# Biases in two buffers, and a block-recursive solve queued behind the last maxima and under high priority, in a two-layer transformer kernel

## The chip, the cores and the metric

One Trainium2 chip, one of its cores. The time is what the device takes for one execution of the program, in microseconds (us); runs of one program are compared by their median. The engines of a core run side by side, each through its own list of instructions and in that list's order: TensorE (PE, with its weight loads PEld), VectorE (DVE), ScalarE (ACT), GpSimd (POOL) and SyncE (SP, which here only issues transfers). They wait for each other by semaphores.

## What is computed

Two blocks, on 256 positions of width 1024. The first block has a pooling layer and a stick-breaking attention layer, each with a memory attention and a gated feed-forward network. The second block is the part that the change touches. It projects its input to columns, of which some feed a block attention with a distance bias ("moba"), some an RWKV recurrence, and some two gates:

```python
u = _rms_norm(h, g_pre[i])
cols = u @ w_in[i]
...
y_a = _moba_attention(qa, ka, va, rel_bias) * silu(za)
y_b, z_b = _rwkv7_time_mix(b_cols, ...)
y_b = y_b * silu(z_b)
merged = (sigmoid(gate_a) * (y_a @ p_a[i]) + sigmoid(gate_b) * (y_b @ p_b[i]))
y = merged @ w_out[i]
h = h + _rms_norm(y, g_post[i])
h = h + sigmoid(h @ w_ple_gate[i]) * (p[i] @ w_ple_up[i])
```

The recurrence, `state = state * w + (state @ a) b + v k`, read out by `r`, is defined step by step over the 256 positions; its output goes through a norm over each head.

## The kernel before

The positions are two tiles of 128 (t = 0 and t = 1). Each tile's whole path is a Python generator (`stream`), and `advance` and `follow` take a step of one or the other in turn, so that both tiles use a block of weights while it is on the chip. A block of weights (`granule`, 256 rows of 512 columns) is loaded by SP into `raw` (four buffers), split by ACT into a rounded part `whi` (line 219) and by DVE into the rest `wlo` (line 220); three matmuls of 512 columns (lines 233 to 235, `acc`) then do one product in full precision. So PE can go on only if DVE and ACT keep splitting, and SP loads the next block only when DVE has read the old one.

The recurrence is done in blocks and not step by step. `rwkv` is a third generator, `side`, of which `aside` takes two steps for each step of tile 0 once the shifted columns are done. It forms strictly lower triangular matrices, one for each head (`rwkv_base`, PE at line 1048); their 32x32 diagonal blocks go through DRAM to POOL, which inverts them all in 30 steps of a multiplication and an addition (`rwkv_blocks`, lines 1069 and 1070), and come back through DRAM as `X` (line 1113). `rwkv_inverse` transposes `X` on DVE into `Z` (lines 1115 and 1116) and joins the 32x32 inverses into 64x64 ones (PE at 1122 and 1130, copies at 1125 and 1132). `rwkv_solve` then solves with them (1188, 1194, 1200) and adds the parts of the output (1208 to 1241), and `rwkv_out` is the norm (1248 to 1261), whose result `yr` is needed by the product with `p_b`.

The block attention (`moba`) runs once for each tile and within it for two groups of four heads. A group loads its distance biases (line 891), forms four tiles of scores (PE, 901), adds biases and takes the row maxima (DVE, 902), negates the maxima (903), takes exponentials (ACT, 906), transposes (PE, 911), copies (912), multiplies by the values (PE, 917) and scales (921).

The order of the instructions on each engine is set by a scheduler that goes by the order of the program, by priority, and by its own estimate of when inputs are there. A wait of an instruction holds up everything behind it on its engine. `behind(a, b)` asks for `a` to stand after `b`, without a wait.

Of the kernel before, what the change touches and what calls it, by code (L numbers as in the profile page):

```python
# [3 lines left out]

# [6 lines left out]
F32 = mybir.dt.float32  # L11
# [9 lines left out]
P = 128  # L21
# [60 lines left out]
def tile_kernel(ctx: ExitStack, tc: tile.TileContext, I, const, off, out):  # L82
# [220 lines left out]
    def close_pool(name):  # L303
        s_ = left if left and left[-1][0] == name else right
        assert s_[-1][0] == name, (name, s_)
        s_.pop()[1].close()
# [3 lines left out]
    def pool_of(name, side="left"):  # L310
        if name not in pools:
            pools[name] = open_pool(name, side)
        return pools[name]
# [345 lines left out]
    def second(t):  # L659
# [121 lines left out]
            V.scalar_tensor_tensor(gt, gt, 1.0, acc, op0=ALU.add, op1=ALU.mult)  # L781
        merged = gates["ga"]
        if t == NT - 1:
            close_pool("moba")
        yield f"out{t}"
        split_yB()
# [51 lines left out]
    def rwkv():  # L838

        el, eo = pools["elem"], pools["eo"]  # L840
        c = {}
        c["kkc"] = bcast(el, I["k_k_2"][0], 512, "kkc")
        c["kac"] = bcast(el, I["k_a_2"][0], 512, "kac")
        for nm, wn, bn in (("wup", "w_up_2", "w0_2"), ("aup", "a_up_2", "a0_2")):
            c[nm] = el.tile([65, 512], F32, name=nm)
            SP.dma_start(c[nm][:64], I[wn][0])
            SP.dma_start(c[nm][64:65], I[bn])
        c["cinc"] = cload(el, "cinc")
        c["half"] = cload(el, "half")
        for t in range(NT):  # L850
            yield from rwkv_elem(t, el, eo, c)
        close_pool("elem")
        close_pool("rk")
        co = pool_of("core")
        ST = co.tile([P, 4, HD], F32, name="ST")

        shared["mask"] = co.tile([P, 2, P], F32, name="mask")
        for w, op in enumerate((ALU.is_gt, ALU.is_ge)):
            G.affine_select(shared["mask"][:, w], one.to_broadcast([P, P]), pattern=[[1, P]], base=0,
                            channel_multiplier=-1, compare_op=op, fill=0.0)  # L860
        for t in range(NT):
            rwkv_base(t, co)
            yield
        rwkv_blocks(co)

        for t in range(NT):
            for tok in zip_longest(*[rwkv_factors(t, g, co) for g in range(2)]):
                if "turn" not in tok:
                    yield
            yield from rwkv_sides(t, co, ST)  # L870
        for _ in zip_longest(*[rwkv_inverse(t, co) for t in range(NT)]):
            yield
        for _ in zip_longest(*[rwkv_solve(t, co, ST) for t in range(NT)]):
            yield
        for t in range(NT):
            yield from rwkv_out(t, co)
            flags.add(f"out{t}")
        close_pool("core")
        close_pool("eo")
        flags.add("core")  # L880

    def moba(t, mo):
        ns = P * (t + 1)
        s0 = P * (1 - t)
        kT_, va = shared["bkT"], bva
        den = sm.tile([P, 8], F32, name="bden")
        mx = sm.tile([P, 8], F32, name="bmx")
        for g in range(2):

            bias = mo.tile([P, 4, T], F32, name="bias")  # L890
            SP.dma_start(bias, bass.AP(tensor=sk.tensor, offset=sk.offset + 127 + g * TOEP,
                                        ap=[[PITCH - 1, P], [2 * TOEP, 4], [1, T]]))
            pm = bias[:, :, s0:]

            for h in range(4):
                hh = 2 * h + g
                o = 64 * g
                if h % 2 == 0:
                    sc = ptr.tile([P, 512], F32, name="tr")
                sv = sc[:, (h % 2) * 256:(h % 2) * 256 + ns]  # L900
                PE.matmul(sv, bq[t][o:o + 64, h], kT_[o:o + 64, h, :ns], start=True, stop=True)
                V.tensor_tensor_reduce(pm[:, h], sv, pm[:, h], 1.0, -3e38, ALU.add, ALU.max, mx[:, hh:hh + 1])
            V.tensor_scalar(mx[:, g:8:2], mx[:, g:8:2], -1.0, None, op0=ALU.mult)
            for h in range(4):
                hh = 2 * h + g
                S.activation(pm[:, h], pm[:, h], AF.Exp, bias=mx[:, hh:hh + 1], accum_out=den[:, hh:hh + 1])
            pT = mo.tile([P, 2, 4, P], F32, name="bPT")
            for j in range(t + 1):
                ps = ptr.tile([P, 512], F32, name="tr")
                for h in range(4):  # L910
                    PE.transpose(ps[:, h * P:(h + 1) * P], pm[:, h, j * P:(j + 1) * P], ident)
                (S.copy if j else V.tensor_copy)(pT[:, j], ps.rearrange("p (a b) -> p a b", a=4))
            po = ptr.tile([P, 512], F32, name="tr")
            for h in range(4):
                hh = 2 * h + g
                for j in range(t + 1):
                    PE.matmul(po[:, h * HD:h * HD + HD], pT[:, j, h], va[j][:, hh * HD:hh * HD + HD],
                              start=(j == 0), stop=(j == t))
            rd = sm.tile([P, 4], F32, name="brd")
            V.reciprocal(rd, den[:, g:8:2])  # L920
            V.tensor_mul(by[t].rearrange("p (h two d) -> p h two d", h=4, two=2)[:, :, g],
                         po[:, :256].rearrange("p (h d) -> p h d", h=4), rd[:, :, None].to_broadcast([P, 4, HD]))
        V.tensor_mul(by[t], by[t], sza[t])
# [183 lines left out]
    def rwkv_inverse(t, co):  # L1107

        d = E[t]
        X = co.tile([P, 8, 32], F32, name="X", bufs=2)  # L1110
        Z = d["Z"] = co.tile([P, 8, 64], F32, name=f"Z{t}")
        G.memset(Z, 0.0)
        G.dma_start(X, of_rows(xsk[t]))
        for n in range(0, P, 64):
            V.transpose(Z[n:n + 32, :, 0:32], X[n:n + 32])
            V.transpose(Z[n + 32:n + 64, :, 32:64], X[n + 32:n + 64])
        yield
        T1 = co.tile([P, 8, 32], F32, name=f"Ld{t}")
        pt = aux(t)
        for h in range(8):  # L1120
            for n in range(0, P, 64):
                PE.matmul(pt[n:n + 32, h * 32:h * 32 + 32], d["Lc"][n + 32:n + 64, h], Z[n + 32:n + 64, h, 32:64],
                          start=True, stop=True)
        for n in range(0, P, 64):
            (S.copy if n else V.tensor_copy)(T1[n:n + 32], pt[n:n + 32, :256].rearrange("p (a b) -> p a b", a=8))
        yield
        px = aux(t)
        for h in range(8):
            for n in range(0, P, 64):
                PE.matmul(px[n:n + 32, h * 32:h * 32 + 32], X[n:n + 32, h], T1[n:n + 32, h], start=True, stop=True)  # L1130
        for n in range(0, P, 64):
            (S.copy if n else V.tensor_copy)(Z[n:n + 32, :, 32:64], px[n:n + 32, :256].rearrange("p (a b) -> p a b", a=8))
        yield
# [8 lines left out]
    def rwkv_sides(t, co, ST):  # L1142

        d = E[t]
        v = vz[t]
        d["rhs"] = co.tile([P, 8, HD * (t + 1)], F32, name=f"rhs{t}")
        if t:
            pa = aux(1)
            for h in range(4):
                PE.transpose(pa[:, h * P:(h + 1) * P], d["AR"][:, h, 0], ident)  # L1150
            S.copy(d["rhs"][:, :, HD:].rearrange("p (g h) e -> p h g e", g=2),
                   pa.rearrange("p (h g e) -> p h g e", h=4, g=2))
        pr = aux(0)
        for k in range(8):
            PE.matmul(pr[:, k * HD:k * HD + HD], d["KM", k // 4][:, k % 4, 0], v[:, head_cols(k)], start=True, stop=True)
        S.copy(d["rhs"][:, :, :HD], pr.rearrange("p (k e) -> p k e", k=8))
        yield
        py = aux(1)
        for k in range(8):
            PE.matmul(py[:, k * HD:k * HD + HD], d["KM", k // 4][:, k % 4, 1], v[:, head_cols(k)], start=True, stop=True)  # L1160
        S.copy(yr[t].rearrange("p h g e -> p g h e"), py.rearrange("p (g h e) -> p g h e", g=2, h=4))
        yield
        if t == 0:
            pS = aux(0)
            for k in range(8):
                o = 64 * (k // 4)
                PE.matmul(pS[o:o + 64, (k % 4) * HD:(k % 4) * HD + HD], d["kt"][:, head_cols(k)], v[:, head_cols(k)],
                          start=True, stop=True)
            S.copy(ST, pS[:, :256].rearrange("p (a b) -> p a b", a=4))
            yield  # L1170
# [104 lines left out]

    def aside(n):

        return sum(1 for _ in zip(range(n), side))

    def advance(t):  # L1280

# [68 lines left out]
```

## Time and profile before

| | us |
|---|---|
| runs shown, median (lowest, highest) | 981.4 (980.11, 981.53) |
| the profiled execution, its own time | 978.99 |
| its span in the trace | 977.3 |
| PE busy in the span | 930.1 |
| DVE busy | 589.3 |
| ACT busy | 509.5 |
| POOL busy | 115.7 |

The trace has a row for each instruction: start, duration, engine, line, operation, what it writes and reads, and, in brackets, how long its engine stood idle before it and what ended that. A granted clock of 1.00 is PE's higher level (2.4 GHz), 0.50 its lower (1.2 GHz).

### The profile page before, as it was taken

The numbers are of one execution on the slowest core, as the hardware profiler recorded it, in microseconds if no ns is written. First come the engines' busy times: TensorE is split into PE (matmuls) and PEld (weight loads), VectorE is DVE, ScalarE is ACT, GpSimd is POOL, SyncE is SP. The second block draws the span as 40 slices with busy tenths as digits, with TensorE's granted clock in tenths as the row PEclk, the third lists the DMA queues.
The fourth block names the chain that finished last, engine by engine and source line by source line (L and its number), as shares of the span: only waits on it lengthen the run. The fifth ranks groups of instructions, "written<-read, shape, count | busy, mean of one in ns | idle before, by whom it ended". The sixth has DMA issues, their size and how long they took to land.

```text
span 977.3 us, 12773 instructions
## 1 busy us (share of the span) xinstructions
PE 930.1 (95%) x4594; PEld 728.2 (75%) x4594; DVE 589.3 (60%) x1002; ACT 509.5 (52%) x883; POOL 115.7 (12%) x220
## 2 busy tenths in 40 slices
PE   8999999999999999999999999798989939999998
PEld 5777788888887777778888888566667727877776
DVE  4754666656666555566656667455997522466864
ACT  5752655555556786665555555454466312435542
POOL 3000200000002000020000000611435840000000
PEclk9999999999999999999999999899999955979999
DMA  7652566565655523456555655555435321235551
GB/s 268 237 185 65 152 197 190 190 184 187 194 175 170 153 84 104 149 185 195 185 185 188 193 178 163 152 153 148 126 117 136 107 53 34 66 120 176 186 175 44
DMA packets 105855, 150.22 MB, mean 154 GB/s; under 512 B 6840, under 2 KB 61214, under 8 KB 105792
## 3 DMA queue, kind: packets, MB, share of 16 engines
q1 hardware_dynamic: 104836, 147.54, 48.0%
q0 software_dynamic: 384, 1.05, 0.5%
q10 hardware_dynamic: 572, 0.82, 0.4%
q8 instruction: 36, 0.59, 0.3%
q14 instruction: 27, 0.22, 0.1%
HBM read 146.24 MB, written 3.15 MB: 153 GB/s over the span
## 4 chain that ended last, share of the span: by engine, by line
PE 75%; POOL 7%; issue 6%; DVE 6%; ACT 3%; DMA 3%; SPq 0%; ACTq 0%; DVEq 0%; POOLq 0%
PE acc L233 16%; PE acc L234 15%; PE acc L235 15%; PE aux L233 5%; PE aux L234 5%; PE aux L235 5%; PE tr L274 2%; DVE wlo L220 2%; POOL Lb L1070 2%; POOL tb L1069 2%; POOL col L711 1%; PE aux L564 1%; POOL rs_w L155 1%; ACT whi L219 1%; DMA x<-in_x_dram 1%
## 5 line engine op out<-in xcount | busy, mean ns | idle before, releaser
L220 DVE SCALAR_TENSOR_TENSOR wlo<-raw,gcol,whi 128x512 fp32r<-128x512 f32 (+1 forms) x364 | 269.0, 768 | 126.9 <-ACT whi L219 126.3
L219 ACT ACTIVATE whi<-raw,gcol 128x512 fp32r<-128x512 f32 (+1 forms) x364 | 243.2, 709 | 182.7 <-PE acc L235 100.7
L233 PE MATMUL acc<-whi,fTh 128*128 128x512 f32 x352 | 141.7, 402 | 0.1
L234 PE MATMUL acc<-wlo,fTh 128*128 128x512 f32 x352 | 137.7, 391 | 1.4 <-DVE wlo L220 1.4
L215 DVE TENSOR_TENSOR wlo<-raw,whi 128x1024 fp32r<-128x1024 f32 x80 | 97.6, 1224 | 66.6 <-ACT whi L214 66.1
L235 PE MATMUL acc<-whi,fTl 128*128 128x512 f32 x352 | 136.9, 390 | 0.0
L214 ACT ACTIVATE whi<-raw 128x1024 fp32r<-128x1024 f32 x80 | 84.7, 1060 | 76.0 <-PE acc L235 71.7
L234 PEld LDWEIGHTS acc<-wlo,fTh 128*128 128x128 f32 x352 | 66.3, 188 | 14.3 <-DVE wlo L220 2.2
L235 PEld LDWEIGHTS acc<-whi,fTl 128*128 128x128 f32 x352 | 66.1, 188 | 14.2
L233 PEld LDWEIGHTS acc<-whi,fTh 128*128 128x128 f32 x352 | 66.1, 188 | 13.9 <-ACT fTh L263 1.4
L233 PE MATMUL acc<-whi,actTh 128*128 128x512 f32 x176 | 72.4, 414 | 1.1 <-ACT actTh L263 0.8
L234 PE MATMUL acc<-wlo,actTh 128*128 128x512 f32 x176 | 70.5, 401 | 0.1
L235 PE MATMUL acc<-whi,actTl 128*128 128x512 f32 x176 | 69.8, 399 | 0.1
L234 PE MATMUL aux<-wlo,hTh 128*128 128x512 f32 x176 | 68.8, 391 | 0.0
L235 PE MATMUL aux<-whi,hTl 128*128 128x512 f32 x176 | 68.7, 390 | 0.0
L233 PE MATMUL aux<-whi,hTh 128*128 128x512 f32 x176 | 68.6, 392 | 0.0
L234 PE MATMUL acc<-wlo,act20h 128*128 128x512 f32 (+1 forms) x104 | 42.7, 411 | 3.7 <-DVE wlo L220 3.7
L233 PE MATMUL acc<-whi,act20h 128*128 128x512 f32 (+1 forms) x104 | 44.6, 429 | 0.0
L233 PE MATMUL acc<-whi,act21h 128*128 128x512 f32 (+1 forms) x104 | 44.2, 425 | 0.0
L234 PE MATMUL acc<-wlo,act21h 128*128 128x512 f32 (+1 forms) x104 | 42.0, 404 | 0.0
L235 PE MATMUL acc<-whi,act21l 128*128 128x512 f32 (+1 forms) x104 | 41.8, 402 | 0.0
L235 PE MATMUL acc<-whi,act20l 128*128 128x512 f32 (+1 forms) x104 | 41.3, 397 | 0.0
(405 smaller groups left out, 1531.8 us busy)
## 6 DMA issues: line engine op xcount, KB each, us to landing
raw<-in_a_w_gu_dram SPq DMA_DIRECT2D x88, 256.0 KB, 3.2
raw<-in_b_w_gu_dram SPq DMA_DIRECT2D x88, 256.0 KB, 3.2
raw<-in_w_in_dram SPq DMA_DIRECT2D x44, 512.0 KB, 3.7
raw<-in_a_w_down_dram SPq DMA_DIRECT2D x22, 512.0 KB, 3.8
raw<-in_b_w_down_dram SPq DMA_DIRECT2D x22, 512.0 KB, 3.7
raw<-in_a_w_out_dram SPq DMA_DIRECT2D x8, 512.0 KB, 3.7
raw<-in_w_kv_dram SPq DMA_DIRECT2D x8, 512.0 KB
raw<-in_b_w_q_dram SPq DMA_DIRECT2D x8, 512.0 KB, 4.3
```

The costliest lines, as they stand in the source:

```text
L155: V.tensor_scalar(w, y, y, h, op0=ALU.mult, op1=ALU.mult)
L214: S.activation(hi[:, :m], raw[:, :m], AF.Copy)
L215: V.tensor_sub(lo[:, :m], raw[:, :m], hi[:, :m].bitcast(F32))
L219: shared["hi"] = S.activation(hi[:, a], raw[:, a], AF.Copy, scale=g)
L220: V.scalar_tensor_tensor(lo[:, a], raw[:, a], g, hi[:, a].bitcast(F32), op0=ALU.mult, op1=ALU.subtract)
L233: PE.matmul(acc, ah[:, k], wh[:, kk], start=first, stop=False)
L234: PE.matmul(acc, ah[:, k], wl[:, kk], start=False, stop=False)
L235: PE.matmul(acc, al[:, k], wh[:, kk], start=False, stop=last)
L274: PE.transpose(ps[:, c * P:(c + 1) * P], src[:, c * P:(c + 1) * P], ident)
L564: PE.matmul(z[:, h * P:(h + 1) * P], kT[j][o:o + 64, p0 + h], qT[t][o:o + 64, p0 + h], start=(h == 0), stop=False, skip_group_check=True)
L1069: G.tensor_mul(tv, Lb[:, j + 1:, j:j + 1].to_broadcast([64, n, j]), Lb[:, j:j + 1, :j].to_broadcast([64, n, j]))
L1070: G.tensor_add(Lb[:, j + 1:, :j], Lb[:, j + 1:, :j], tv)
```

## The change

Four things. The generator of the recurrence waits, ahead of its last part, until the second tile's last group of maxima has been written in the program; from there on every step taken by `aside` is under the scheduler's high priority. The eight transposes of `X` are put `behind` the negation of those last maxima. The second tile loads the biases of both groups at its start, the second group's into a buffer of its own in a new pool. That pool is closed ahead of the attention's.

```diff
         if t == NT - 1:
+            close_pool("bias")
             close_pool("moba")
...
             yield from rwkv_sides(t, co, ST)
+
+        while "maxima" not in shared:
+            yield
+        flags.add("urgent")
+        yield
         for _ in zip_longest(*[rwkv_inverse(t, co) for t in range(NT)]):
             yield
...
+        def bias_of(g):
+
+            bias = (pool_of("bias", "right") if t and g else mo).tile([P, 4, T], F32, name="bias")
+            SP.dma_start(bias, bass.AP(tensor=sk.tensor, offset=sk.offset + 127 + g * TOEP,
+                                       ap=[[PITCH - 1, P], [2 * TOEP, 4], [1, T]]))
+            return bias
+
+        both = [bias_of(g) for g in range(2)] if t else None
         for g in range(2):
-
-            bias = mo.tile([P, 4, T], F32, name="bias")
-            SP.dma_start(bias, bass.AP(tensor=sk.tensor, offset=sk.offset + 127 + g * TOEP,
-                                        ap=[[PITCH - 1, P], [2 * TOEP, 4], [1, T]]))
-            pm = bias[:, :, s0:]
+            pm = (both[g] if t else bias_of(g))[:, :, s0:]
...
-            V.tensor_scalar(mx[:, g:8:2], mx[:, g:8:2], -1.0, None, op0=ALU.mult)
+            last = V.tensor_scalar(mx[:, g:8:2], mx[:, g:8:2], -1.0, None, op0=ALU.mult)
+            if t and g:
+                shared["maxima"] = last
...
-            V.transpose(Z[n:n + 32, :, 0:32], X[n:n + 32])
-            V.transpose(Z[n + 32:n + 64, :, 32:64], X[n + 32:n + 64])
+            behind(V.transpose(Z[n:n + 32, :, 0:32], X[n:n + 32]), shared["maxima"])
+            behind(V.transpose(Z[n + 32:n + 64, :, 32:64], X[n + 32:n + 64]), shared["maxima"])
...
     def aside(n):
 
-        return sum(1 for _ in zip(range(n), side))
+        for _ in range(n):
+            with tc.high_priority() if "urgent" in flags else nullcontext():
+                if next(side, "end") == "end":
+                    return
```

Three places show what this does to the lists. Lines from 783 on have other numbers in the changed program: 902 is 912 there, 903 is 913, 912 is 924, 921 is 933, 1115 and 1116 are 1127 and 1128, 1188 is 1200, 1194 is 1206, 1200 is 1212, 1211 is 1223, 972 is 984, 979 is 991 and 991 is 1003.

The first is DVE's list at the first group of the second tile's maxima (`bmx` are the maxima, `Z_7174` the first tile's transposed inverses, `wlo` the split of a weight block). Before:

```order
L902 ISA bias,bmx<-tr,bias 128x256
L902 ISA bmx 128x1
L902 ISA bias,bmx<-tr,bias 128x256
L902 ISA bmx 128x1
L1115 STREAM_TRANSPOSE Z_7174<-X 32x8x32
L902 ISA bias,bmx<-tr,bias 128x256
L902 ISA bmx 128x1
L1116 STREAM_TRANSPOSE Z_7174<-X 32x8x32
L902 ISA bias,bmx<-tr,bias 128x256
L902 ISA bmx 128x1
L1115 STREAM_TRANSPOSE Z_7174<-X 32x8x32
L903 TENSOR_SCALAR bmx<-bmx 128x4
```

Now, from the end of that group on (its four maxima stand ahead of these rows):

```order
L913 TENSOR_SCALAR bmx<-bmx 128x4
L220 SCALAR_TENSOR_TENSOR wlo<-raw,gcol,whi 128x512
L932 RECIPROCAL brd<-bden 128x4
L924 COPY bPT<-tr 128x512
L933 TENSOR_TENSOR by_5582<-tr,brd 128x4x64
L220 SCALAR_TENSOR_TENSOR wlo<-raw,gcol,whi 128x512
L912 ISA bias,bmx<-tr,bias 128x256
...
L913 TENSOR_SCALAR bmx<-bmx 128x4
L1127 STREAM_TRANSPOSE Z_7197<-X 32x8x32
L1128 STREAM_TRANSPOSE Z_7197<-X 32x8x32
```

The transposes stood between the second and the third maximum of the first group; now they stand behind the second group's maxima, with the first group's copy, scaling and two weight splits ahead of them. The seven rows at the left out place are the read of that group's first maximum and its three other maxima with their reads.

The second place is PE's list in the solve (`rhs`, `Z`, `KM`, `Lb`, `N` are tiles of the solve, `acc` the gates' products). Before:

```order
L1188 MATMUL aux_7308<-rhs_6892,Z_7174 64x64 x8
L1188 MATMUL aux_7319<-rhs_7124,Z_7182 64x128 x4
L1188 MATMUL aux_7325<-rhs_7124,Z_7182 64x128 x4
L1194 MATMUL aux_7331<-KM_7307,N_6793 64x64 x4
L1194 MATMUL aux_7331<-KM_7307,N_6795 64x64 x4
L1194 MATMUL aux_7341<-Lb,N_7120 64x128 x4
L233 MATMUL acc<-whi,act21h 128x512
L234 MATMUL acc<-wlo,act21h 128x512
L1194 MATMUL aux_7347<-Lb,N_7122 64x128 x4
L235 MATMUL acc<-whi,act21l 128x512
```

Now:

```order
L1206 MATMUL aux_7356<-KM_7310,N_6793 64x64 x4
L1206 MATMUL aux_7356<-KM_7310,N_6795 64x64 x4
L1200 MATMUL aux_7322<-rhs_7127,Z_7205 64x128 x4
L1212 MATMUL aux_7378<-rhs_6892,Z_7197 64x64 x8
L1200 MATMUL aux_7328<-rhs_7127,Z_7205 64x128 x3
L1206 MATMUL aux_7366<-Lb,N_7123 64x128 x4
L1200 MATMUL aux_7328<-rhs_7127,Z_7205 64x128
L234 MATMUL acc<-wlo,act21h 128x512
```

The solve's third step (1200, now 1212) follows within the rows of its first two, where before ten `acc` matmuls stood ahead of it. Between the first matmul of the joins and the last of the solve stand 33 `acc` matmuls now and 36 before; from behind the second tile's first scores (901) to the first transposes of `by` (274) both lists hold the same 374 matmuls, 158 of them `acc`.

The third place is DVE's list some 60 us earlier, at the decays of the second tile (`ms` is the sum of two small vectors that the solve uses late). Before:

```order
L1005 TENSOR_REDUCE bon_6471<-sq 128x8
L220 SCALAR_TENSOR_TENSOR wlo<-raw,gcol,whi 128x512 x2
L1014 COPY AR_6502<-aux_6505 128x4x128
L220 SCALAR_TENSOR_TENSOR wlo<-raw,gcol,whi 128x512 x2
L1211 TENSOR_TENSOR ms_7406<-mid_6144,mid_6399 128x16
L220 SCALAR_TENSOR_TENSOR wlo<-raw,gcol,whi 128x512 x2
```

Now:

```order
L991 COPY mid_6399<-aux_6394 128x16
L1003 SCALAR_TENSOR_TENSOR k_6439<-k_6439,rk_5584 128x512
L1223 TENSOR_TENSOR ms_7431<-mid_6144,mid_6399 128x16
L984 TENSOR_TENSOR prev<-aux_6385,col 128x512
L1009 TENSOR_TENSOR bt<-bt,col 128x512
L220 SCALAR_TENSOR_TENSOR wlo<-raw,gcol,whi 128x512
```

The sum now stands two rows behind the copy that it needs; its exponential (line 1212) moves the same way on ACT. On SP's list, the second group's biases move ahead of four weight loads that stood before the first tile's second biases.

## Rows read from the trace of the kernel before

**Rows 1.** The page: span, busy time of PE, its clock in 40 slices.

```profile
span 977.3 us, 12773 instructions
...
PE 930.1 (95%) x4594; PEld 728.2 (75%) x4594; DVE 589.3 (60%) x1002; ACT 509.5 (52%) x883; POOL 115.7 (12%) x220
...
PEclk9999999999999999999999999899999955979999
```

**Rows 2.** Busy time by stretch: length, PE, PEld, DVE, ACT, POOL, granted clock, DMA share, GB/s.

```profile
782.60:800.00 17.40, 0.50 (x11) 0.37 (x11) 2.88 (x10) 0.68 (x3) 9.97 (x23) 0.59 0.12 30
800.00:826.70 26.70, 26.70 (x94) 21.04 (x95) 7.38 (x21) 8.27 (x23) 0.00 (x0) 0.50 0.20 59
826.70:857.40 30.70, 30.70 (x351) 25.46 (x349) 14.10 (x23) 12.03 (x21) 0.00 (x0) 1.00 0.24 70
857.40:867.60 10.20, 10.20 (x31) 8.11 (x30) 3.75 (x10) 1.96 (x3) 0.00 (x0) 0.50 0.00 0
867.60:886.00 18.40, 18.40 (x81) 14.80 (x80) 16.18 (x44) 10.80 (x16) 0.00 (x0) 1.00 0.61 202
886.00:977.30 91.30, 84.19 (x377) 65.29 (x375) 60.45 (x91) 40.45 (x57) 0.00 (x0) 1.00 0.42 141
```

**Rows 3.** Waits of DVE and PE from 777 to 800: total, times, longest.

```profile
DVE Z L1115 <- DMA X<-xsk: 18.8, 1, 18.8
...
PE tr L911 <- ACT bias L906: 16.9, 1, 16.9
```

**Rows 4.** Instructions in order of time, all engines, 782 to 800: start, duration.

```profile
782.02 0.57 PE L235 MATMUL acc<-whi,act20l 128*128 128x512 f32 x1
...
790.69 0.24 POOL L1070 TENSOR_TENSOR Lb<-Lb,tb 64x30 f32<-64x30 f32 x1
...
793.75 1.85 POOL L1113 DMA_DIRECT2D X<-xsk  x2 [1.48 <-DMA xsk<-Lb]
796.95 0.43 DVE L1115 STREAM_TRANSPOSE Z<-X 32x256 f32<-32x256 f32 x1 [18.81 <-DMA X<-xsk]
...
799.12 0.17 DVE L903 TENSOR_SCALAR bmx<-bmx 128x4 f32<-128x4 f32 x1
...
799.98 0.69 PE L911 MATMUL tr<-ident,bias 128*128 128x128 f32 x2 [16.90 <-ACT bias L906]
```

**Rows 5.** Instructions in order of time, 804 to 886.5.

```profile
804.06 0.37 SPq L891 DMA_DIRECT2D bias<-skew  x1
...
808.06 3.08 PE L917 MATMUL tr<-bva,bPT 128*128 128x64 f32 x14
...
816.10 2.07 PE L901 MATMUL tr<-bkT,bqT 64*128 64x256 f32 x4
...
819.38 0.16 DVE L903 TENSOR_SCALAR bmx<-bmx 128x4 f32<-128x4 f32 x1
...
828.40 1.96 PE L917 MATMUL tr<-bva,bPT 128*128 128x64 f32 x16
...
840.31 0.69 DVE L1195 TENSOR_TENSOR rhs<-rhs,aux 64x512 f32<-64x512 f32 x1 [2.00 <-PE aux L1194]
...
862.40 0.69 PE L1236 MATMUL aux<-ST,KM 64*128 64x64 f32 x2
...
886.04 0.60 PE L274 MATMUL tr<-ident,by 128*128 128x128 f32 x4
```

**Rows 6.** The early sum on DVE, its exponential on ACT, in order of time.

```profile
733.50 1.25 DVE L1211 TENSOR_TENSOR ms<-mid,mid 128x16 f32<-128x16 f32 x1
...
734.79 0.22 ACT L1212 ACTIVATE ms<-ms 128x16 f32<-128x16 f32 x1 [2.61 <-DVE ms L1211]
```

**Rows 7.** Busy time by stretch, as rows 2, around that sum.

```profile
730.00:740.00 10.00, 9.03 (x53) 6.64 (x55) 9.10 (x10) 4.41 (x8) 9.36 (x9) 1.00 0.42 111
```

**Rows 8.** POOL's additions with DVE at work and with DVE idle, in order of time.

```profile
771.64 1.19 POOL L1070 TENSOR_TENSOR Lb<-Lb,tb 64x240 f32<-64x240 f32 x1
...
778.90 0.62 POOL L1070 TENSOR_TENSOR Lb<-Lb,tb 64x228 f32<-64x228 f32 x1
```

More of the change, by code (lines that the diff above doesn't have):

```diff
@@ L1 @@
 import math
-from contextlib import ExitStack
+from contextlib import ExitStack, nullcontext
 from itertools import zip_longest
```

## The prediction

> **What bounds the kernel now.** First the page: PE is busy for 930.1 of 977.3 us and no other engine comes near it [rows 1], so time is to be had only where PE stands idle or where it is paid at the lower clock. The row of the clock shows where: its 40 slices of 24.4 us read 8 or 9, and only the 33rd to 36th, some 782 to 880 us, read 5, 5, 9, 7. The busy time by stretch resolves it [rows 2]: from 782.60 to 800.00 PE works for 0.50 of 17.40 us; then it is busy without a gap up to 886.00, but 26.70 and 10.20 us of that are at a granted clock of 0.50, and only 30.70 and 18.40 us at 1.00. Behind 886 come 91.3 us at 1.00.
>
> The waits say what the hole is [rows 3]: DVE waits once, 18.8 us, at line 1115 for the load of `X`, and PE once, 16.9 us, at line 911 for ACT's exponentials (906). The instructions in order of time join the two [rows 4]. `X` comes from POOL's inversion, whose last addition starts at 790.69; its load is issued at 793.75, and the transpose starts at 796.95. It stands in DVE's list in the middle of the first group's maxima, so the last maxima wait behind it, line 903 ends at 799.29, and PE's next matmul starts at 799.98. PE's previous one ended at 782.59. Nothing in that group needs `X`: this wait is order alone.
>
> The sum is made against the profiled execution, 978.99 us, of which 977.3 are the span; this lies 2.4 under the median of the runs, 981.4, and the result is carried over to that median.
>
> **The change, part by part.** The lists hold the same 374 matmuls between the same two points, and the lists behind the transposes of `by` stand as before. So the new time is the old one, less the idle time that goes, plus new waits, plus or minus what the clock does.
>
> *A. The transposes of `X` behind the last maxima.* The hole, 782.59 to 799.98, less what must stay of it. DVE has the first group's last two maxima left (it did those in the 2.2 us between 797.4 and 799.3 [rows 4]), which it now does as soon as the scores are there, beside PE's work. I take the whole, 17.2 us off. What is late next? `X` still lands at about 797. Before, from PE's restart to the negation of the second group's maxima (819.38) were 19.4 us, at the lower clock throughout [rows 5]: the first group's transposes, 14 of its products in 3.08, the second group's scores in 2.07. Started from 782.6 with the same rows, the second maxima end at 797 to 802, so the transposes of `X` behind them find it there or a microsecond short of it. Wait for `X` at DVE: 0 to 1, hidden by the first group's weight splits ahead. What is queued there if it is longer: the second group's copies and splits, so PE at once.
>
> *B. High priority: the sum `ms`.* Before, line 1211 took 1.25 us on DVE at 733.50, and ACT stood 2.61 us for it [rows 6]; now it stands two rows behind the copy that it needs. But PE idled for only 0.97 of the 10 us around it [rows 7]. I take −0.7, between −1.0 and 0.
>
> *C. POOL beside a working DVE.* Before, POOL's last 24 instructions (12 steps) ran from 778.90 to 790.93, mostly while DVE stood still. Its additions took 0.62 us with DVE idle (778.90) and 1.19 of nearly the same shape with DVE at work (771.64) [rows 8]. If all 12 additions are slowed by that 0.57, `X` comes 6.8 us later, at 804; if none, at 797. The later ones are small (64x30 in 0.24), so I take 1 to 2 us for `X`, which costs 0 to 1 of the end, as the maxima are not over before: +0.5.
> The Trainium skill, *SBUF — State Buffer*, section "Who interferes with whom", says that a DVE instruction with two inputs in SBUF and a GpSimd instruction that reads SBUF exclude each other for their whole length. This speaks against the change; by it the some three weight splits that now fall into the loop's last 12 us would hold POOL for two us or so, and the two additions above agree with such a hold.
>
> *D. The second bias buffer.* Before, the second group's biases were issued at 804.06, when the first group's had been read out [rows 5]. With one buffer that load would sit in the new path; with two it is issued tens of us earlier, behind four weight loads fewer on SP's queue. Cost 0: those loads come one place later, and PE's products have raw blocks in hand (DMA share 0.42 there [rows 7], far from full). If that cover is gone, it is one load's few us, once.
>
> *E. The denser solve.* High priority pulls the third solve step into the first two, and 33 instead of 36 `acc` stand between the first join and the last step. Each step is a hop PE, DVE, PE like that at 840.31, where DVE took 0.69 us and PE was kept at work by fillers [rows 5, 2]. Below, 0 (PE had no gap there before, and 33 of 36 fillers remain); above, the cover of about 12 hops lost by 0.69 each, 8 us. I take +2, nearer to the row without gaps.
>
> *F. The clock.* It decides the size. The same kind of product (917) costs 3.08/14 = 0.220 us at 0.50 and 1.96/16 = 0.1225 at 1.00 [rows 5]: a us at the lower level buys 0.56 us of work, and 44% of it is lost. Of the 36.9 us at 0.50, then, 16.4 are loss. Before, the clock fell in the hole [rows 2]. Without the hole it need not; yet it stayed at 0.50 through 26.7 us of work without a gap, and fell again at 857.4 while PE was busy without one. So idle time alone doesn't set it; what ran in these stretches were transposes and narrow products, and the change keeps all of those and packs the solve's more closely. I take the lower clock for as long as before: 0. Bounds: only 15 of the 36.9 us remain, −9.7; or half from 782.6 until the joins and solve are over, some 50 us, +5.9.
>
> Sum: −17.2 − 0.7 + 0.5 + 2 + 0 = −15.4: 963.6 on the profiled execution's time, **966.0** on the median. Then `by`'s first transposes, 886.04 before [rows 5], start at about 870.
>
> **The rivals.**
> *The clock comes back early, or never falls.* With −9.7 for F the gain is 22 to 28: 953 to 959. For it: the hole that preceded the fall is gone. Against: the two stretches at 0.50 with a PE that was 100% busy. The Trainium skill, *TensorE: Matmul & The Clock Gate*, section "What's actually happening", says that the default is throttled and that activity releases it; by that rule alone the hole would have cost both its 17 us and the 16.4 of loss behind it, and the time would be 950. The rows agree with it for the fall in the hole, and not for the 26.7 us behind it. Chance 0.17.
> *The dense chain waits.* `X` at 804 and DVE held for 5 us at its transposes, with the second group's copies and the splits behind them, or the solve's hops open to 8 us: the gain shrinks to 3 to 10, 971 to 978. For it: 12 additions at 1.19. Against: the shrinking shapes, and no gap in PE's work through the solve before [rows 2]. Chance 0.13.
> *The clock stays low: slower.* The solve's narrow products now follow more closely and from about 800 on; if the clock stays at 0.50 from 782.6 on through everything up to `by`, the 49.1 us at 1.00 become 49.1 × 1.8 = 88, and the time is 39 − 15.4 = 24 above now, 1005. It decides when the extra time at 0.50 exceeds 15.4/0.44 = 35 us, that is when the clock doesn't return before about 855. Against: behind the solve's last product (862.40), wide products brought it back by 867.6 [rows 5, 2], and now there are more of these left for the end. Chance 0.05.
> *Nothing changes*, because the gain is given back by a wait in the last 91 us, 979 to 983: the tail's own rows [rows 2] show 7 us of PE idle that a differently timed load could stretch. Chance 0.05. That the change doesn't do what it says is excluded: the lists show the transposes moved.
>
> **How the numbers follow.** The likeliest case, a gain of 10 to 22 (959 to 971), has 0.60; the sum's 966.0 lies in it. The range takes in the early clock and half of the dense chain: 953.0 to 975.0; outside are the slow clock and no change (0.10), the upper half of the dense chain (0.05) and a clock at 1.00 throughout (0.03). About 0.2%, 2 us, is what a measurement of this kernel can tell from no change. Faster: 0.60 + 0.17 + 0.13 and a little of the no-change case, 0.91; same 0.03; slower 0.05 and a little, 0.06.
>
> **What would show it.** A: no stretch of 17 us without PE and DVE at 780 to 800; the wait for `X` at the transpose (now 1127) under 2 us; the last negation at 797 to 802, not 819.4. B: the sum at about the time of that copy, and no wait of 2.6 us on ACT. C: POOL's last addition at 791 to 793. E: PE without gaps over a us between the joins and the last solve step. F: some 37 us at 0.50 between 782 and `by`; fewer than 15 or more than 50 would make the prediction wrong in size, over 72 in sign. `by` at about 870, and 91 us behind it as before; a longer tail would make it wrong by that.

## The result and the profile after

| | median, us | lowest to highest | runs |
|---|---|---|---|
| before | 983.13 | 980.11 to 986.0 | 10 |
| changed | 977.24 | 970.88 to 978.84 | 10 |

The ratio is 0.9935, 95% interval 0.9914 to 0.9956: faster by 0.65%, some 6 us, where 15 were forecast. A ratio leaves out runs that lie over 1.5% above the fastest of their kernel, which matters most for the kernel with one bias buffer below, where one short run of 965.31 puts three of six outside.

The profiled execution of the changed kernel took 978.78 us, nearly as long as the one of before (978.99), so the two traces can't be laid side by side by their ends. First its page, as [rows 1]:

```profile
span 977.1 us, 12775 instructions
...
PE 940.8 (96%) x4594; PEld 735.7 (75%) x4594; DVE 590.3 (60%) x1002; ACT 509.4 (52%) x883; POOL 116.5 (12%) x220
...
PEclk9997999999999999999999999999989995799999
```

The row of the clock has a 7 in its fourth slice that [rows 1] does not have. Busy time by stretch (columns as [rows 2]) of the changed kernel, with two stretches far ahead of the attention:

```profile
50.00:100.00 50.00, 49.54 (x276) 37.47 (x274) 22.43 (x40) 18.62 (x44) 0.50 (x2) 0.90 0.35 109
700.00:750.00 50.00, 47.17 (x234) 35.79 (x234) 44.56 (x71) 27.19 (x53) 22.73 (x18) 0.93 0.36 107
782.60:799.10 16.50, 14.71 (x89) 10.52 (x88) 8.30 (x26) 7.09 (x21) 14.25 (x29) 1.00 0.23 65
799.10:805.30 6.20, 0.00 (x0) 0.02 (x1) 0.97 (x3) 1.67 (x6) 2.42 (x4) 0.89 0.35 85
805.30:844.50 39.20, 39.19 (x302) 32.90 (x303) 12.10 (x25) 7.35 (x14) 0.00 (x0) 0.50 0.05 14
844.50:857.80 13.30, 13.30 (x72) 9.94 (x70) 5.16 (x13) 3.35 (x6) 0.00 (x0) 0.98 0.27 80
857.80:861.90 4.10, 4.10 (x14) 3.19 (x14) 2.36 (x8) 1.33 (x2) 0.00 (x0) 0.59 0.00 0
861.90:885.60 23.70, 23.70 (x105) 19.09 (x104) 18.07 (x40) 14.13 (x21) 0.00 (x0) 1.00 0.65 206
885.60:977.10 91.50, 84.12 (x377) 65.27 (x375) 60.59 (x91) 40.33 (x57) 0.00 (x0) 0.99 0.42 139
```

The same two early stretches before:

```profile
50.00:100.00 50.00, 49.55 (x294) 38.14 (x293) 25.23 (x44) 20.65 (x47) 0.50 (x2) 1.00 0.40 128
700.00:750.00 50.00, 46.25 (x253) 34.40 (x253) 44.54 (x73) 29.45 (x59) 25.19 (x21) 1.00 0.43 120
```

From 50 to 100 us PE is as busy in both, on work that the change does not touch, but at a clock of 0.90 here and 1.00 there; 700 to 750 is alike (0.93 and 1.00). Together that puts the changed trace some 8 us behind. The first fall, 80.3 to 90.6 at 0.50, is chance of the execution, and it is the trace of before that is the exception: eleven of the thirteen profiles of this document have a fall there, that of before with the short loop among them. The second, 718.6 to 725.5, comes on the same matmuls behind the same two waits (1.21 and 0.73 us) that run at 1.00 before; it is in the five profiles of kernels with two bias buffers and the transposes behind the maxima and in no other, and whether it is chance is not shown. So stretches are compared from a common point: the first matmuls of `rwkv_base` for the second tile (1083, now 1095) start at 743.97 before and at 750.68 now, 6.7 us later, and the first transposes of `by` at 886.04 before [rows 5] and 885.58 now, 0.5 earlier. Between the two the change gains 7.2 us; the tail behind is 91.3 us before [rows 2] and 91.5 now.

Where the hole went is in the waits of the changed kernel (engine, line, what ended the wait; total, times, longest), as [rows 3]:

```profile
PE aux L1134 <- DVE Z L1128: 6.2, 1, 6.2
...
DVE Z L1127 <- DMA X<-xsk: 6.2, 1, 6.2
```

and in its instructions in order of time, as [rows 4]:

```profile
797.84 0.20 DVE L913 TENSOR_SCALAR bmx<-bmx 128x4 f32<-128x4 f32 x1
...
798.10 0.25 POOL L1082 TENSOR_TENSOR Lb<-Lb,tb 64x30 f32<-64x30 f32 x1
...
798.76 0.31 PE L923 MATMUL tr<-ident,bias 128*128 128x128 f32 x1
...
804.29 0.43 DVE L1127 STREAM_TRANSPOSE Z<-X 32x256 f32<-32x256 f32 x1 [6.24 <-DMA X<-xsk]
...
805.32 0.28 PE L1134 MATMUL aux<-Z,Lc 32*32 32x32 f32 x2 [6.25 <-DVE Z L1128]
```

The second maxima are negated at 798.04, 6.2 us ahead of `X`. DVE reaches the transposes and stands; PE, whose list has a join right behind one transpose of the attention, stands behind it. So a hole of 17.4 us, in which PE waited 16.9 [rows 2, 3], became a wait of 6.2, and the stretch at 0.50 behind it, 26.7 us before, became 39.2, in which PE is busy without a gap.

### The profile page after: what moved, and what is told of

Read it like the earlier page. It is cut to its first block, busy times and chain, and to the rows that moved or that the text cites. A ratio compares the mean times of both kernels' runs of the same rounds, so it can differ in the third digit from the quotient of the medians.

```text
span 977.1 us, 12775 instructions
## 1 busy us (share of the span) xinstructions
PE 940.8 (96%) x4594; PEld 735.7 (75%) x4594; DVE 590.3 (60%) x1002; ACT 509.4 (52%) x883; POOL 116.5 (12%) x220
## 4 chain that ended last, share of the span: by engine, by line
PE 77%; POOL 7%; issue 6%; DVE 4%; ACT 3%; DMA 3%; SPq 0%; DVEq 0%; ACTq 0%; POOLq 0%
PE acc L233 16%; PE acc L234 16%; PE acc L235 16%; PE aux L233 5%; PE aux L234 5%; PE aux L235 5%; PE tr L274 2%; POOL Lb L1082 2%; POOL tb L1081 2%; DVE wlo L220 2%; POOL col L711 1%; PE aux L564 1%; PE tr L507 1%; POOL rs_w L155 1%; PE aux L1246 1%
```

## Experiments

Each was timed beside the kernel before, whose medians in the three groups were 983.1, 983.8 and 983.3.

**Without the high priority.** The change less one line:

```diff
-        flags.add("urgent")
```

> The change without its high priority: the recurrence still waits for the last maxima, the transposes of X still stand behind them, the biases still have two buffers. In the lists the joins stand as one block behind twelve acc products, and 6 to 12 acc products stand between the steps of the solve. Theory 1 (the wait for X that is left, 6.2 us in the profile after, is the whole of what the change misses): the acc products cover it, about 971 us, and the time at a clock of 0.50 stays at 35 to 45 us. Theory 2 (the solve's narrow products, drawn together by the high priority, hold the clock down): the 43 us or so at 0.50 shrink below 20, which gives another 10 us, about 960. Rival: without priority the solve ends later, the product with p_b waits for yr, and the time is that of the change, 977, or longer.

966.18 us, ratio 0.9837 [0.9792, 0.9882]: 11 us faster than the change. Its busy time by stretch:

```profile
806.30:812.20 5.90, 0.05 (x2) 0.07 (x1) 4.51 (x11) 0.00 (x0) 0.00 (x0) 0.75 0.09 24
812.20:819.30 7.10, 7.10 (x27) 6.52 (x28) 2.37 (x4) 0.59 (x1) 0.00 (x0) 0.50 0.28 76
819.30:850.00 30.70, 30.70 (x341) 24.71 (x339) 13.12 (x23) 11.60 (x20) 0.00 (x0) 1.00 0.24 69
```

The hole is still there, 5.9 us (now PE waits for the second group's copy, which stands behind the transposes on DVE), so theory 1's part, that the `acc` would cover it, failed. But the clock is back after 7.1 us instead of 39.2, the last 3 of them `acc` products, which is theory 2's part; its 960 is missed by the hole that stayed.

**High priority from the solve on.** The flag is set behind the loop of the joins:

```diff
-        flags.add("urgent")
-        yield
         for _ in zip_longest(*[rwkv_inverse(t, co) for t in range(NT)]):
             yield
+        flags.add("urgent")
+        yield
```

> High priority begins only behind the joins, so that the joins stand behind twelve acc products as without it, and the solve is as dense as in the change. Theory 1: PE's wait of 6.2 us for the joins shrinks to 3 or so, 972 to 975. Theory 2: the same wait shrinks, but the clock still falls in the solve and stays at 0.50 for 30 to 45 us; if this kernel is over 5 us slower than the one with no priority at all, it is the dense solve that costs.

969.84 us, ratio 0.9875 [0.9832, 0.9918]. Six of its runs lie between 967.88 and 971.34 at mean clocks of 0.973 to 0.978; the profiled one took 977.38 at 0.965, with some 41 us at 0.50 from 760 to 900 (worked out from the granted clock of each 2 us), as in the change. So the same lists can give either. The 3.7 us over the kernel with no priority lie inside the intervals: this one tells nothing alone.

**The loop of POOL cut, with the change and before it.** The last 12 of the 30 steps are left out, so the inverses are not complete.

```diff
-        for j in range(1, 31):
+        for j in range(1, 19):
```

> The change with POOL's inversion cut from 30 steps to its first 18 (the inverses are then not complete, so the output isn't the reference's): X lands some 12 us earlier, so nothing waits for it. Theory 1: the 6.2 us go and no more, 971. If the idle stretch is what brings the clock down, the 40 us at 0.50 behind it go too, and the time is 950 to 955. Theory 2: the clock falls all the same when the solve begins, with 30 us or more at 0.50, and the time is 965 to 971.

> The kernel before with the same cut of POOL's loop to 18 steps (the output isn't the reference's). If the wait at DVE's transpose is all that the change is about, X some 12 us earlier takes 12 of its 18.8 us: 971 us, and with the cut the change gains only what is left, 5 us. If the time at 0.50 hangs on the length of the idle stretch, it shrinks too, and the time is below 965.

With the change 963.98, ratio 0.9805 [0.9758, 0.9853]. No wait for `X` is left in its trace, and the clock falls all the same, but briefly:

```profile
790.60:821.00 30.40, 30.01 (x342) 23.73 (x340) 13.28 (x33) 12.53 (x31) 1.84 (x2) 0.97 0.16 45
821.00:828.00 7.00, 7.00 (x38) 5.69 (x37) 3.04 (x7) 1.47 (x3) 0.00 (x0) 0.64 0.00 0
828.00:839.00 11.00, 11.00 (x55) 7.96 (x54) 4.88 (x11) 3.57 (x6) 0.00 (x0) 0.92 0.17 49
839.00:850.20 11.20, 11.20 (x35) 8.90 (x36) 4.45 (x15) 2.03 (x3) 0.00 (x0) 0.55 0.21 53
```

The joins and the first two steps of the solve, which the change ran at 0.50, run here at the higher level, as densely; the clock falls only in what follows them. That is neither theory's case: some 17 us at 0.50, where theory 1 had none or 40 and theory 2 had 30 or more. Taking the 6.2 us away was worth 13.

Before the change 972.55, ratio 0.9899 [0.9853, 0.9946]. This one did not do what was meant: the scheduler knew of the shorter loop and moved the transposes forward in DVE's list, so that PE still stood 15.2 us (from 776.4 to 791.56). It gained 10.6 us nevertheless, and the stretches say how:

```profile
778.00:794.50 16.50, 2.94 (x11) 2.75 (x12) 5.06 (x11) 0.39 (x1) 7.07 (x12) 0.53 0.14 34
794.50:800.50 6.00, 5.51 (x28) 3.62 (x27) 4.99 (x11) 0.00 (x0) 0.00 (x0) 0.86 0.09 11
800.50:850.00 49.50, 49.45 (x470) 40.11 (x471) 22.95 (x52) 21.97 (x48) 0.00 (x0) 1.00 0.29 85
```

Here the hole ends ahead of eight narrow products, four `acc` and the 256 column products of `KM`, and the clock is back five us later. A hole nearly as long as that of before was followed by 26.7 us at 0.50 there and some five here (791.56 to about 796).

**High priority for the joins alone.**

```diff
+        flags.discard("urgent")
+        yield
         for _ in zip_longest(*[rwkv_solve(t, co, ST) for t in range(NT)]):
```

> High priority for the joins alone, taken back ahead of the solve: PE's list is the change's up to the joins (the wait of 6.2 us for X with them), and behind them up to 30 acc products stand together and between the steps of the solve. Theory 2 (the dense solve holds the clock at 0.50): the time at 0.50 falls from 43 to about 20 us, and the time is 967. Theory 1 (the clock follows the idle stretch alone, which is unchanged): 40 us at 0.50 and 975 to 978.

961.41, ratio 0.9784 [0.975, 0.9818]. The list of PE is that of the change through the hole; behind the joins stand the `acc`:

```profile
797.90:802.90 5.00, 0.09 (x1) 0.00 (x0) 0.87 (x2) 1.79 (x7) 1.85 (x2) 0.73 0.33 83
802.90:807.10 4.20, 4.07 (x42) 3.36 (x43) 3.88 (x10) 0.40 (x1) 0.00 (x0) 0.51 0.00 0
807.10:844.60 37.50, 37.50 (x361) 31.71 (x360) 16.15 (x28) 14.37 (x25) 0.00 (x0) 1.00 0.29 85
```

After nearly the same hole (5.0 us) 4.2 us at 0.50 instead of 39.2, and all six runs, 956.08 to 968.41, are shorter than the shortest of the change. That the `acc` brought the clock back is not shown by this trace: it is back at 807.1, behind the same matmuls with the same three `acc` that the change runs from 805.3 to 809.5 at 0.50, and the 36 `acc` that stand together come only from 813.4 to 821.9.

**The order taken away, the priority kept.**

```diff
-            behind(V.transpose(Z[n:n + 32, :, 0:32], X[n:n + 32]), shared["maxima"])
+            V.transpose(Z[n:n + 32, :, 0:32], X[n:n + 32])
```

The second transpose likewise.

> The change with its high priority and two bias buffers, but without the order that puts X's transposes behind the maxima: in DVE's list all eight of them now stand ahead of the masks KM and of both groups' maxima. They then wait for X for 20 us or more with nearly everything of DVE behind them: a longer hole than before, 985 to 1000. If the order does not matter, 977.

993.53, ratio 1.0093 [1.006, 1.0126], slower than before. Its waits:

```profile
PE aux L1113 <- DVE KM L1107: 23.6, 1, 23.6
DVE Z L1127 <- DMA X<-xsk: 22.1, 1, 22.1
```

So the change's gain in the hole is the order's; the priority by itself pulls the transposes further forward.

**One bias buffer.** The second group's biases are loaded at its group's start, into the pool of the first:

```diff
-            bias = (pool_of("bias", "right") if t and g else mo).tile([P, 4, T], F32, name="bias")
+            bias = mo.tile([P, 4, T], F32, name="bias")
...
-        both = [bias_of(g) for g in range(2)] if t else None
         for g in range(2):
-            pm = (both[g] if t else bias_of(g))[:, :, s0:]
+            pm = bias_of(g)[:, :, s0:]
```

> The change with one bias buffer, the second group's biases loaded when the first group's have been read out. As the second maxima end 6 us ahead of X, a load of some 3 to 5 us in their path hides in the wait for X: 975 to 979, no difference from the change. If the second buffer matters, 981 or more.

979.87, ratio 0.9877 [0.9821, 0.9932], from runs that lie far apart (965.31 to 982.1). The interval meets the change's only from 0.9914 to 0.9932, on the faster side, while the median lies 2.6 us above the change's: whether the second buffer makes a difference these runs cannot tell. In the trace the second load is issued at 786.95, the second maxima end at 795.26, and `X` is awaited for 4.5 us behind them.

**The transposes behind the scaling of the second group, with each priority.** The instruction that they stand behind is another, the scaling of the second group (933 in the change) instead of its negation (913):

```diff
-            last = V.tensor_scalar(mx[:, g:8:2], mx[:, g:8:2], -1.0, None, op0=ALU.mult)
-            if t and g:
-                shared["maxima"] = last
+            V.tensor_scalar(mx[:, g:8:2], mx[:, g:8:2], -1.0, None, op0=ALU.mult)
...
-            V.tensor_mul(by[t].rearrange("p (h two d) -> p h two d", h=4, two=2)[:, :, g],
+            last = V.tensor_mul(by[t].rearrange("p (h two d) -> p h two d", h=4, two=2)[:, :, g],
                          po[:, :256].rearrange("p (h d) -> p h d", h=4), rd[:, :, None].to_broadcast([P, 4, HD]))
+            if t and g:
+                shared["maxima"] = last
```

Without priority:

> As the kernel without priority, with X's transposes put behind the scaling of the second group's output instead of behind its maxima, so that DVE does the second group's copy, two weight splits and the scaling while X is on its way. If the order at DVE is still what makes the hole, PE's 5.8 us of waiting at the values' product go and with them the clock's fall behind it, some 8 us at 0.50 which are worth 4: 966 - 10 = 956. Rival: the hole moves to the joins or to the end of the solve, and the time stays at 964 to 967.

With the change's priority:

> The change with its high priority throughout, but X's transposes behind the scaling of the second group's output instead of behind its maxima: the solve is as dense as in the change, and PE has the values' products and five acc products ahead of the joins. If it takes the idle stretch and the dense solve together to keep the clock at 0.50 for 40 us, there are about 17 us at 0.50 left, and the time is that of the change with the short loop, 964. If the dense solve alone does it, 970 to 972 with 40 us at 0.50.

With priority for the joins alone:

> High priority for the joins alone and X's transposes behind the scaling. Neither an idle stretch nor a dense solve is left: 953 to 956, with 15 us or less at 0.50. If the position of the transposes adds nothing where the priority ends at the solve, 961 as without it.

| medians, us | behind the maxima (hole) | behind the scaling (none) |
|---|---|---|
| high priority throughout | 977.24 | 956.73 |
| for the joins alone | 961.41 | 955.75 |
| none | 966.18 | 955.28 |

The ratios of the right column are 0.9741 [0.9714, 0.9767], 0.9717 [0.9695, 0.9739] and 0.9719 [0.9694, 0.9744]. Without a hole the priority costs nothing that can be measured; with one it costs 11 us against none. Busy time by stretch of the change with the later place, its high priority kept:

```profile
789.20:823.20 34.00, 33.91 (x366) 26.82 (x365) 14.67 (x35) 12.88 (x29) 10.13 (x22) 0.99 0.23 63
823.20:827.00 3.80, 3.80 (x23) 3.21 (x22) 2.85 (x6) 0.58 (x1) 0.00 (x0) 0.57 0.02 4
827.00:840.70 13.70, 13.70 (x75) 10.30 (x73) 5.51 (x13) 5.04 (x8) 0.00 (x0) 0.99 0.26 77
840.70:847.60 6.90, 6.90 (x19) 5.41 (x19) 4.48 (x14) 1.86 (x3) 0.00 (x0) 0.51 0.04 12
847.60:867.10 19.50, 19.50 (x87) 16.05 (x86) 14.43 (x31) 11.62 (x17) 0.00 (x0) 1.00 0.71 219
```

No hole, and some 10 us at 0.50 where the change has 39.2 and 4.1. The time is below both of the expected ones; from 760 to 890 the 17 us at 0.50 that the first of them named are there.

**The best, with the early sum.** The kernel with no priority and the transposes behind the scaling, its `ms` and exponential put under high priority:

```diff
-            V.tensor_add(ms, E[0]["mid"], E[1]["mid"])
-            S.activation(ms, ms, AF.Exp)
+            with tc.high_priority():
+                V.tensor_add(ms, E[0]["mid"], E[1]["mid"])
+                S.activation(ms, ms, AF.Exp)
```

> No priority but for the sum ms and its exponential, X's transposes behind the scaling. Against the same kernel without the early sum, 955.3: the 1.25 us that DVE loses at the old place and ACT's wait of 2.6 are worth 0.4 to 1.5 us, 954 to 955; if they are hidden, no difference.

953.01, ratio 0.97 [0.9676, 0.9724], against 0.9719 [0.9694, 0.9744] without: 2.3 us that the intervals don't separate. It is the fastest measured, 30 us below before, five times what the change gives.

## Why the prediction failed, point by point

**A, the hole: the step that failed.** The prediction had the second maxima end at 797 to 802, just when `X` lands, by adding up durations of the restart before [rows 5], all taken at 0.50. But that stretch was at 0.50 because of the hole ahead of it. Without the hole it ran at 1.00 (782.60 to 799.10 above), and the maxima ended at 798.04, which is 791.3 on the clock of before's trace (6.7 less). `X` came at 804.29, 797.6 there, 0.6 later than before. The wait for `X` was not 0 to 1 us but 6.2. PE's wait went from 16.9 [rows 3] to 6.2, a gain of 10.7 us, not 17.2; the prediction had also read the hole's start too early, since PE still works for 0.50 us behind 782.60 [rows 2]. What the prediction named as waiting behind it there, copies and splits and so PE, held; PE was stopped even sooner, by a join of its own that the high priority had put at the head of its list. That is the rival "the dense chain waits" in its place and its price (971 to 978, measured 977.24), but with another cause: the maxima early, not `X` late.

**F, the clock: the size.** Taken as the same 36.9 us at 0.50; there were 39.2 + 3.4 of the 4.1, 42.6 us, which is 5.7 more and by 44% a loss of 2.5. The bound of +5.9 held. Before, PE was also busy at 0.50 from 779.0 to 782.3, ahead of the hole, which the prediction did not count and the change does not have; with it the difference is 2.4 us and the loss 1.1. What the prediction missed is why: it weighed "idle" against "narrow products" as rivals, and the table shows that the time is lost where both are there. (Nor were the products at 0.50 before all narrow: among the 94 of the 26.7 us stood 16 `acc`, of 512 columns.) In the profiles, after a hole and in front of the dense solve the clock stays at 0.50 for 39.2 us (49.4 with one bias buffer); after the hole and in front of a looser list for 4.2 or 7.1; in front of the dense solve without a hole (the short loop, the later place) it falls only toward its end. So removing 6.2 us of waiting gave 20.5 (977.24 to 956.73): the 6.2, some 11 from the time at 0.50 from 760 to 890 (about 17 us instead of 42.6, at 44%), and 3 that are not accounted for and lie about the size of the spread between runs. How the two act together is open: with the priority from the solve on, the profiled execution had the clock back 9.4 us behind its hole and, 3.4 us later, at 0.50 again for 23.9 us of joins and solve, while six runs of the same kernel are 6 us or more shorter.

**B, the sum: right, at its bound.** It stands at 729.28 for 0.17 us now. From the last transposes of `btmp` to the first matmuls of `rwkv_base`, 725.71 to 743.97 before and 733.99 to 750.68 now, 18.3 us became 16.7, and 1.6 went, beyond the bound of 1.0. But not all of it is the sum's. The kernels without priority and with priority for the joins alone keep the late sum and have the same low clock just ahead, and take 17.8 there; those with the early sum and without that low clock (the later place with the change's priority, the best) take 17.1. So the sum is worth 1.1, and 0.4 to 0.5 go with the clock ahead of it. The kernel that has it alone against its neighbour gave 2.3 with overlapping intervals.

**C, POOL: right, with a little less than the 1 to 2 us taken.** Its last addition starts at 798.10, 791.4 on before's clock against 790.69 [rows 4]: 0.7 later. On the Trainium skill's rule (*SBUF — State Buffer*, "Who interferes with whom"), two us were named; the trace agrees in kind, with less: two of DVE's weight splits fell into the loop's last 12 us, and the one multiplication beside each took 0.33 us longer than before (0.88 and 0.74 against 0.55 and 0.41), which is the 0.7. The additions, which the prediction reckoned with, are as long as before.

**D, the second buffer: no cost shown, and no gain.** In the one trace with one buffer the second maxima still end 4.5 us ahead of `X`, so a later load has room there; the runs are too far apart to say more.

**E, the denser solve:** no gap of PE, so none of the 8 us. Of the terms, −10.7 for the hole and +1.1 for the clock make −9.6, and measured between the common points are −7.2; the rest, 2.4, is what E, taken as +2, and the readings' rounding may share. No run isolates it.

**The sum.** On the traces the change is worth 1.1 + 7.2 − 0.2 = 8.1 us; the medians say 5.9, with an interval that reaches to 8.5. That the two profiled executions are level comes from the lower clock far ahead of it; were the fall at 718.6 the change's own, its some 3 us (6.8 at 44%) would bring the 8.1 to about the medians' figure. The clock that stays low, the rival on the other side, had its chance for a reason: the longer time at 0.50 is there, and ate 1.1 of the 10.7 us that the hole gave.

## What to carry to other kernels

A duration read behind a hole is a duration at the clock that the hole left; before adding such rows up for a version without the hole, they have to be turned into the higher level, and what they then reach earlier may wait again. When a wait can't be removed, look at what stands behind it: here holes of 5 to 6 us cost 4 to 7 us at 0.50 in front of one list and 39.2 in front of a denser one of the same work. And an order that puts a waiting instruction behind the last producer that comes in time should be carried on until the awaited data are there: one group of work further was worth 20 us, over three times the change.

## What the runs showed of the hardware

Runs of one kernel differ by the clock they are granted, in places that no edit touches. The changed kernel took 970.88 us at a mean clock of 0.971 and 978.84 at 0.962; 0.009 of the span at half rate stands for 17.5 us at 0.50, which at 44% is 7.7 of the 8.0 us between them. A profiled execution is one draw of these, and can hide a difference of 8 us. Nor does a list alone fix the clock: one run of the kernel with one bias buffer took 965.31 at a mean clock of 0.980, the other five 976.64 to 982.1, at 0.961 to 0.965.

A PE that is busy without a gap does not get the higher clock by that: 39.2 us at 100% busy stayed at 0.50. Within them stood 15 `acc` products, 7.98 us. The Trainium skill, *TensorE: Matmul & The Clock Gate*, "What's actually happening", says that activity releases the throttle; the traces without priority and of before with the short loop agree, with the clock back 7.1 and 4.6 us behind the hole, after a few `acc` products; that of the change does not, for 39.2 us.
